# Hybrid attention layer on one core: part of the second token half's input projection goes from whole columns beside attention to seven-product blocks ahead of it, and the rest runs in held half columns

## The chip, the cores and the metric

The kernel runs on one core of a Trainium2 chip. The metric is the device time of one execution in microseconds (us). The median of three runs of the kernel before is 2537.37 us (2536.17 to 2539.38).

## The reference, cut to what matters

One layer of a streaming encoder works on 2048 tokens of width 1024, all in fp32. Its first part is what the change touches:

```python
u = rms_norm(h, g_mix_pre[l])
z = u @ w_in[l]                       # 1024 x 2816
qa, ka, va, qh, fh, ih, gh = jnp.split(z, IN_SPLITS, axis=-1)
ya = swa_with_sinks(qa, ka, va, sinks[l])     # 8 heads, sliding window of 128
yh = hgrn2(qh, fh, ih, gh, lb, onorm)         # 4 heads, gated recurrence
y = jnp.concatenate([ya, yh], axis=-1) @ w_out[l]
h = h + rms_norm(y, g_mix_post[l])
```

Cross-attention into 256 memory tokens and a SwiGLU network follow; they are not touched. The 2816 columns of `w_in` are 22 column groups of 128: 0 to 3 are `qa`, 4 `ka`, 5 `va`, 6 to 9 `qh`, 10 to 13 `fh`, 14 to 17 `ih`, 18 to 21 `gh`.

## The kernel before

**Arithmetic.** An fp32 operand is split into a rounded part and a rest (`hi`, `lo`), and each product of 128 x 128 by 128 x 512 becomes three matmuls, hi by hi, hi by lo, lo by hi (`mm3` L156 to L158, `products` L1198 to L1200). A split is a copy on ScalarE (ACT, L1035) or GpSimd (POOL, L1037) and a subtraction on VectorE (DVE, L1038).

**Blocks.** For a pair of column groups and 1024 tokens the product is a 2 x 2 block product. `plain` and `eight` form it with eight half-size products (96 matmuls of 512 columns), `seven` with seven (84), at the price of sums of the weights (`streamed`, L1173), of sums of the tokens' blocks (`resident`, keys 5, 7, 6, 4), and of sums of results. `phases` runs lists of such blocks; the token operands `T` of a list lie in seven tiles, four of the pool `big` and three of the pool `tb`, each split in two halves (`half`, `split`), and stay for the whole list.

**Stage 1, `in_first`.** The first 1024 tokens are normalised and go through the eleven pairs of `ORDER`: two plainly, nine in seven products. Beside these blocks the second 1024 tokens are normalised and stored to `un_d`. At the end they are fetched, split into four plain tiles of `big` (`u1`), and the pair (4, 5) of the second half is done plainly. `in_block.after` finishes a pair: for `fh` and `qh` (pairs (10, 6) to (13, 9)) it runs `decays` (logarithm, two scans, exponentials, L790 to L814), and then stores the pair to `z_d`, or to `zq_d`, `zk_d`.

**Stage 2, attention.** `mix` steps through three generators. `swa` does tile n's scores and softmax (`swa_front`: scores L859, L860, masked minimum on DVE L864, exponential on ACT L868, division L879) and tile n-1's output (`swa_back`: transposes L893, ACT copy L897, DVE difference L898, matmuls L902, L903). `hgrn` does the recurrence: `hgrn_last` L994, `hgrn_out` L976 and L977 (then ACT squares L981, POOL L983 and L985, DVE L986), `hgrn_state` L965, `hgrn_front` L938 (scores), POOL L946, transposes L949 and L954. `cols` (`in_proj`, `in_cols`) does the remaining 20 column groups of the second half, one per step, 48 matmuls each, with loads (`wcols`) and splits. Nine steps run all three; in the eight after them `swa` runs with `cols` and with the sums of `w_out` (`side`, DVE L1082); the rest of `cols` runs with `fold_cross`.

**PSUM.** In stage 2 there are eight banks in four kinds of two: `g` for the column groups, `s` and `t` for `swa` (with `h` from tile 8 on), and `h` for the recurrence of tiles 0 to 7. A bank is used again when its reader has finished.

**Order.** Each engine, and SyncE (SP) with the DMA issues, executes one list in order. A scheduler makes the lists when the program is built, from the order in which the code is traced and from which operands it takes to be ready; `queued(i)` puts what is traced within it behind the instruction i. So the column matmuls of `cols`, which wait for nothing but their weights, could be put anywhere between the attention matmuls.

Of the kernel before, what the change touches and what calls it, by code (L numbers as in the profile page):

```python
# [18 lines left out]
P = 128  # L19
T = 2048  # L20
# [28 lines left out]
class Layer:  # L49
# [146 lines left out]
    def mix(self):  # L196
        tc, I = self.tc, self.I
        kw = dict(reuse_waits="tile")
        with contextlib.ExitStack() as left:
# [18 lines left out]
            with tc.tile_pool(name="sw", bufs=1, side="right", **kw) as self.sw:  # L218
# [216 lines left out]

    ORDER = [(4, 5), (0, 1), (2, 3)] + [(10 + h, 6 + h) for h in range(4)] + [(c, c + 1) for c in range(14, 22, 2)]
# [31 lines left out]
    def in_first(self):  # L468
# [63 lines left out]
        second = {}  # L532

        def fetch():
            for s in range(2):
                for q in range(2):
                    r = self.pair_tile().rearrange("p a d -> p (a d)")
                    self.load(r.rearrange("p (n c) -> p n c", n=4),
                              self.un_d[4 * s:4 * s + 4, q].rearrange("n p c -> p n c"))
                    second[q, s] = r.rearrange("p (m k c) -> p k m c", m=16, k=4)  # L540
                    yield

        beside = [(), (0,), (1, 2), (3,), (4,), (5,), (6,), (7,), (), (), (), ()]
        get = fetch()
        tokens = [[] for _ in range(len(self.ORDER) + 1)]
        blocks = [("s",) + self.in_block(*p, tokens[i], tokens[i + 1], beside[i + 1], get if i > 9 else (), i < 2,
                                         None if i else lambda: x_loads(0, (2, 3)))
                  for i, p in enumerate(self.ORDER)]

# [3 lines left out]
        phases = self.phases([(lambda i, j, a, n: raw[i, j][:, a:a + n, :], 4, blocks, None, {})], T)  # L553
# [46 lines left out]
        for _ in get:  # L600
            pass
        u = []
        for s in range(2):
            u.append([])
            for q in range(2):
                self._n += 1
                t = self.big.tile([P, 2, 4, 512], F32R, tag="big", name=f"u1_{q}{s}")
                r = second[q, s]
                for k in (0, 2):
                    self.split2(r[:, k:k + 2], *(t[:, e, k:k + 2].rearrange("p k (m c) -> p k m c", m=16)  # L610
                                                 for e in range(2)), "A")
                u[s] += [(t[:, 0, k, :], t[:, 1, k, :]) for k in range(4)]

        c0 = self.ORDER[0][0] * P

        def load(t, j):
            for i, c in enumerate(self.ORDER[0]):
                self.load(t[:, :, i * P:(i + 1) * P], I["w_in"][c, :, 4 * j:4 * j + 4, :])

        stream = self.streamed(load, 4, "p")  # L620
        next(stream)
        S = list(stream)
        z, low = self.pair_tile(), self.pair_tile()
        for s in range(2):
            sl = slice(s * 512, (s + 1) * 512)
            for i in range(2):
                ps = self.bank("g")
                self.mm3(ps, [((S[i + k // 4 * 2][:, 0, k % 4, :], S[i + k // 4 * 2][:, 1, k % 4, :]), u[s][k])
                              for k in range(KT)])
                if i:  # L630
                    nc.scalar.activation(z[:, i, sl], ps, AF.Copy)
                else:
                    self.halves(c0, ps, z[:, 0, sl], low[:, 0, sl])
        self.store_halves(c0, TB, z[:, 0, :], low[:, 0, :])
        self.store(self.z_d[c0 + P:c0 + 2 * P, TB:2 * TB], z[:, 1, :])
        return u
# [13 lines left out]
    def in_block(self, ca, cb, x, ahead, beside, get, plain, between):  # L650
# [11 lines left out]
        def stream(kind):  # L662
            for _ in range(3):
                next(iter(get), None)
            return self.streamed(load, 4, kind)

        def out(i, j, a, b):
# [15 lines left out]
            if c0 < C_VA:  # L683
# [3 lines left out]
                if b is not None:  # L687
                    nc.vector.tensor_tensor(lo, a, b, ALU.add)
# [4 lines left out]
            if b is not None:  # L693
                nc.vector.tensor_tensor(zs, a, b, ALU.add)
                a = zs
            if c0 < C_QH or C_IH <= c0 < C_GH:
                if b is None:
# [11 lines left out]
        def after():  # L709
# [7 lines left out]
            if C_FH <= c0 < C_IH:  # L717
                e = self.pair_tile()
                yield from self.decays(0, (c0 - C_FH) // P, z[0][:, 0, :], e[:, 0, :], e[:, 1, :])
# [4 lines left out]
            for i, c in enumerate(() if plain else (ca, cb)):  # L724
                if c0 < C_VA:
                    self.store_halves(c * P, 0, z[1][:, i, :], z[0][:, i, :])
                else:
                    self.store(self.z_d[c * P:(c + 1) * P, 0:TB], z[0][:, i, :])
# [8 lines left out]
    def in_proj(self, b, u):  # L737

        order = [c for p in self.ORDER for c in p]
        e1 = None  # L740
        for c in order[2:]:
# [1121 lines left out]
```

## Time and profile before

| | us |
|---|---|
| median of 3 runs | 2537.37 |
| the profiled execution, its own time | 2533.9 |
| its span, first to last instruction | 2532.2 |
| busy, in the span: TensorE (PE) | 2493.8 |
| VectorE (DVE) | 1749.1 |
| ScalarE (ACT) | 1240.7 |
| GpSimd (POOL) | 365.4 |

Granted clock of TensorE: 0.998 over the span. Times in views are counted from the span's start. In them stage 1 ends at about 269 us (the blocks of the first half reach to 244.5, the plain pair of the second half to 269), attention at about 603, and `fold_cross` at about 764. A row of a timeline has start, duration, engine, line, operation, output<-input, shape, count, and in brackets the idle time before it with what ended it. A row of a group has its count after x, then the busy time in us, the mean of one in ns, and the idle time before.

### The profile page before, as it was taken

What the parts mean: (1) busy time and instruction counts of PE and PEld (TensorE: products, weight loads), DVE (VectorE), ACT (ScalarE), POOL (GpSimd) and SP (SyncE); (2) the same over time, 40 slices, a digit from 0 to 9 for tenths busy, and PEclk for the clock granted to TensorE, in tenths of its full rate; (3) what the DMA queues carried; (4) which work ended last, traced back from release to release, by engine and by line L of the source; (5) the groups of instructions that cost most, each with busy time, mean ns of one, the idle gap of its engine ahead of it and who ended that gap; (6) DMA issues with size and microseconds to landing.
All of it is one profiled execution on the core that took longest, in us unless ns stands there. A gap on an engine that the chain in (4) does not pass through costs nothing.

```text
span 2532.2 us, 33939 instructions
## 1 busy us (share of the span) xinstructions
PE 2493.8 (98%) x11942; PEld 2084.7 (82%) x11942; DVE 1749.1 (69%) x2787; ACT 1240.7 (49%) x2582; POOL 365.4 (14%) x540
## 2 busy tenths in 40 slices
PE   9999999999999999999999999999999999999998
PEld 8778888888987788878878888888888888888886
DVE  8896477865556989988866655576566557574766
ACT  5463356654565576566753333353333335443543
POOL 4241244321400111112200000000000000000122
PEclk9999999999999999999999999999999999999999
DMA  7544877785887996858944322254354334565777
GB/s 221 158 158 164 239 198 178 223 270 135 278 298 266 302 335 194 255 175 255 339 164 169 136 76 93 78 196 154 129 208 167 117 127 156 177 184 110 231 169 156
DMA packets 313403, 483.56 MB, mean 191 GB/s; under 512 B 21904, under 2 KB 198032, under 8 KB 313232
## 3 DMA queue, kind: packets, MB, share of 16 engines
q1 hardware_dynamic: 304880, 455.17, 54.1%
q0 software_dynamic: 8352, 26.22, 6.1%
q8 instruction: 94, 1.54, 0.2%
q14 instruction: 77, 0.63, 0.1%
HBM read 305.15 MB, written 176.16 MB: 190 GB/s over the span
## 4 chain that ended last, share of the span: by engine, by line
PE 83%; DVE 5%; DMA 5%; issue 2%; ACT 2%; POOL 1%; SPq 1%; DVEq 0%; POOLq 0%; ACTq 0%
PE psm L1200 22%; PE psm L1198 22%; PE psm L1199 22%; PE psg L158 2%; PE psg L156 2%; PE psg L157 2%; DVE S L1038 1%; DMA y_d<-ys 1%; DVE T L1038 1%; DMA raw<-in_wo_x_dram 1%; DVE sum L1173 0%; DMA pair<-in_x_dram 0%; DMA out_s<-u 0%; SPq L75 0%; ACT junk L1569 0%
## 5 line engine op out<-in xcount | busy, mean ns | idle before, releaser
L1198 PE MATMUL psm<-T,S 128*128 128x512 f32 x2680 | 1034.4, 391 | 12.6 <-ACT part L1213 8.4
L1199 PE MATMUL psm<-T,S 128*128 128x512 f32 x2680 | 1042.6, 390 | 1.2 <-DVE T L1038 1.1
L1200 PE MATMUL psm<-T,S 128*128 128x512 f32 x2680 | 1030.0, 390 | 5.0 <-DVE S L1038 5.0
L1198 PEld LDWEIGHTS psm<-T,S 128*128 128x128 f32 x2680 | 503.1, 188 | 124.8 <-ACT part L1213 13.0
L1200 PEld LDWEIGHTS psm<-T,S 128*128 128x128 f32 x2680 | 503.4, 188 | 112.4 <-DVE S L1038 8.4
L1199 PEld LDWEIGHTS psm<-T,S 128*128 128x128 f32 x2680 | 503.5, 188 | 106.7 <-DVE T L1038 3.0
L1035 ACT ACTIVATE S<-sum 128x512 fp32r<-128x512 f32 (+1 forms) x370 | 224.1, 619 | 374.8 <-PE psm L1200 270.4
L1038 DVE TENSOR_TENSOR S<-sraw,S 128x512 fp32r<-128x512 f32 (+1 forms) x315 | 212.0, 679 | 236.9 <-ACT S L1035 233.7
L1213 ACT ACTIVATE part<-psm 128x512 f32<-128x512 f32 x285 | 168.6, 596 | 253.1 <-PE psm L1200 237.8
L1038 DVE TENSOR_TENSOR S<-sum,S 128x512 fp32r<-128x512 f32 (+1 forms) x388 | 258.0, 673 | 43.9 <-ACT S L1035 40.0
L1035 ACT ACTIVATE S<-sraw 128x512 fp32r<-128x512 f32 (+1 forms) x300 | 184.5, 618 | 110.7 <-PE psm L1200 108.7
L1602 POOL DMA_DIRECT2D y_d<-row x16 | 14.0, 872 | 1077.3 <-DVE row L1784 1015.3
L1038 DVE TENSOR_TENSOR T<-row,T 128x1024 fp32r<-128x1024 f32 (+1 forms) x112 | 130.8, 1183 | 28.3 <-ACT T L1035 26.4
L156 PE MATMUL psg<-u,whi 128*128 128x512 f32 x320 | 127.6, 399 | 0.7 <-DVE z L770 0.5
L157 PE MATMUL psg<-u,whi 128*128 128x512 f32 x320 | 127.3, 398 | 0.0
L158 PE MATMUL psg<-u,wlo 128*128 128x512 f32 x320 | 126.7, 397 | 0.0
L1569 ACT ACTIVATE junk<-row 128x512 f32<-128x512 f32 x160 | 99.6, 624 | 46.3 <-DVE row L1591 19.9
L1035 ACT ACTIVATE T<-row 128x1024 fp32r<-128x1024 f32 (+1 forms) x112 | 113.4, 1031 | 10.6 <-DMA row<-d_s 5.3
L1735 DVE TENSOR_TENSOR row<-psm,part 128x512 f32<-128x512 f32 x66 | 44.0, 687 | 71.3 <-PE psm L1200 71.3
L1038 DVE TENSOR_TENSOR wlo<-raw,whi 128x1024 fp32r<-128x1024 f32 x52 | 65.4, 1258 | 36.0 <-ACT whi L1035 30.9
L1784 DVE TENSOR_TENSOR row<-psm,part 128x512 f32<-128x512 f32 x72 | 49.1, 687 | 49.3 <-PE psm L1200 49.2
L1744 DVE TENSOR_TENSOR part<-psm,part 128x512 f32<-128x512 f32 x66 | 43.7, 687 | 52.2 <-PE psm L1200 52.2
(355 smaller groups left out, 3476.2 us busy)
## 6 DMA issues: line engine op xcount, KB each, us to landing
sraw<-in_w_gate_dram SPq DMA_DIRECT2D x44, 512.0 KB, 3.8
sraw<-in_w_up_dram SPq DMA_DIRECT2D x44, 512.0 KB, 3.6
hid_d<-row SPq DMA_DIRECT2D x44, 512.0 KB, 2.6
sraw<-hid_d SPq DMA_DIRECT2D x32, 512.0 KB, 4.6
sraw<-in_w_in_dram SPq DMA_DIRECT2D x48, 256.0 KB, 3.9
raw<-in_w_in_dram SPq DMA_DIRECT2D x20, 512.0 KB, 6.3
row<-in_w_down_dram SPq DMA_DIRECT2D x20, 512.0 KB, 7.3
row<-d_s SPq DMA_DIRECT2D x20, 512.0 KB, 8.4
```

The source lines that it names most:

```text
L156: nc.tensor.matmul(ps, ah, bh, start=(i == 0), stop=False)
L157: nc.tensor.matmul(ps, ah, bl, start=False, stop=False)
L158: nc.tensor.matmul(ps, al, bh, start=False, stop=(i == n - 1))
L1035: self.nc.scalar.activation(hi, raw, AF.Copy)
L1038: self.nc.vector.tensor_tensor(lo, raw, f32(hi), ALU.subtract)
L1198: nc.tensor.matmul(ps, s[:, 0, k, :], t[:, 0, k, :], start=st, stop=False, **kw)
L1199: nc.tensor.matmul(ps, s[:, 0, k, :], t[:, 1, k, :], start=False, stop=False, **kw)
L1200: nc.tensor.matmul(ps, s[:, 1, k, :], t[:, 0, k, :], start=False, stop=sp, **kw)
L1213: nc.scalar.activation(t, ps, AF.Copy)
L1569: self.nc.scalar.activation(junk, a, AF.Square, scale=float(D) ** -0.5, accum_out=to)
L1735: nc.vector.tensor_tensor(d, a, c, ALU.add)
L1784: nc.vector.tensor_tensor(d, a, b, ALU.add)
```

## The change

`ORDER` and the first token half stay. A second list of blocks is handed to `phases`: the first five pairs of `ORDER` for the second half, (4, 5), (0, 1), (2, 3) and (10, 6) in seven products, and (11, 7) in eight (kind "p"). Their token operands take over the tiles of the first list one by one, each as soon as its last use there is past. Four tiles of raw tokens are fetched, and the sums 7, 5 and 6 formed, beside the last two blocks of the first half. The 12 column groups that are left use the tiles 1, 2, 8 and 3 of the last block. They run in halves of 24 matmuls: two before the first step, one in each of the first nine steps, one and two by turns in the later ones; each half after the first two is put behind the last TensorE instruction traced before it, which ends the step's `hgrn` (or `swa`).

```diff
-                for _ in range(NPB + 1):
+                next(cols)
+                for i in range(NPB + 1):
                     next(swa)
                     next(hgrn)
+                    self.hold = [self.traced(mybir.EngineType.PE)]
                     next(cols)
...
-                    next(cols)
+                    self.hold = [self.traced(mybir.EngineType.PE)]
+                    for _ in range(1 + i % 2):
+                        next(cols)
...
+    MORE = 5
...
+        more = [("p" if i == self.MORE - 1 else "s",) + self.in_block(*p, 1, (), [], (), False, None)
+                for i, p in enumerate(self.ORDER[:self.MORE])]
...
+        def sums():
+            for k, at in ((7, (1, 1)), (5, (0, 1)), (1, (0, 0)), (2, (1, 0))):
+                second[k] = fetched(*at)
+                yield
+            for d, a, b, op in ((7, 7, 5, ALU.subtract), (5, 5, 1, ALU.subtract), (6, 1, 7, ALU.add)):
...
+                for k in (0, 2):
+                    kk = slice(k, k + 2)
+                    nc.vector.tensor_tensor(second[d][:, kk], second[a][:, kk], second[b][:, kk], op)
+                    yield
...
-        phases = self.phases([(lambda i, j, a, n: raw[i, j][:, a:a + n, :], 4, blocks, None, {})], T)
+        phases = self.phases([(lambda i, j, a, n: raw[i, j][:, a:a + n, :], 4, blocks, None, {len(blocks) - 2: [sums]}),
+                              (operand, 4, more, True, {})], T)
...
-        order = [c for p in self.ORDER for c in p]
+        order = [c for p in self.ORDER for c in p][2 * self.MORE:]
...
         for s in range(TB // 512):
+            if s:
+                yield
...
-                self.mm3(ps, [((w[i][0][:, k, :], w[i][1][:, k, :]), u[s][k]) for k in range(KT)])
+                with self.queued(*self.hold):
+                    self.mm3(ps, [((w[i][0][:, k, :], w[i][1][:, k, :]), u[s][k]) for k in range(KT)])
...
+                if first and queue[0][0]:
+                    free = next(s for s in slots if s[2] == where[queue[0][1]])
```

The plain pair at the end of `in_first`, with its fetches and splits, is removed. In the program 48 matmuls of 512 columns go in all.

Two places show the new order. First TensorE, in one of the first nine steps before, from the last matmul of `hgrn_out` (L977, bank psh) on: `psg` are column matmuls, L893 transposes of the softmax, L902 its product with the values.

```order
L977 MATMUL psh_4143<-W_3880,q_3905 128x128
L893 MATMUL pst_4108<-ident,S_10_3769 128x128 x2
L893 MATMUL pst_4108<-ident,S_11_3779 128x128 x2
L157 MATMUL psg_4212<-u_10_2237,whi_4207 128x512
L158 MATMUL psg_4212<-u_10_2237,wlo_4208 128x512
L156 MATMUL psg_4240<-u_01_2242,whi_4207 128x512
L902 MATMUL pss_4102<-pth_00_4089,vst_3463 128x512
L157 MATMUL psg_4240<-u_01_2242,whi_4207 128x512
L158 MATMUL psg_4240<-u_01_2242,wlo_4208 128x512
L156 MATMUL psg_4240<-u_01_2242,whi_4207 128x512
```

Of the changed program the same engine at the end of the attention part of the same kind of step; its line numbers are nine lower in these functions (L929 are the scores of `hgrn_front`, L940 and L945 its transposes, L884 those of the softmax, L893 the product with the values).

```order
L884 MATMUL pst_4553<-ident,S_00_4240 128x128 x2
L884 MATMUL pst_4553<-ident,S_01_4250 128x128 x2
L929 MATMUL psh_4399<-qq_4394,k_4392 128x192 x2
L884 MATMUL pss_4544<-ident,S_00_4240 128x128 x2
L884 MATMUL pss_4544<-ident,S_01_4250 128x128 x2
L929 MATMUL psh_4404<-qq_4394,k_4392 128x192 x2
L940 MATMUL psh_4412<-ident,k_4392 128x128 x4
L884 MATMUL pst_4568<-ident,S_10_4273 128x128 x2
L884 MATMUL pst_4568<-ident,S_11_4283 128x128 x2
L893 MATMUL pss_4562<-pth_00_4549,vst_4002 128x512
L945 MATMUL psh_4419<-ident,v_4396 128x128 x4
L156 MATMUL psg_4426<-T_2788,whi_3985 128x512
```

The column matmuls, which lay in pieces of one to ten between the attention matmuls, now stand in one piece of 24 behind the step's last transposes; between `hgrn_out` and those there is none.

Second SP before, where attention starts: the loads of the recurrence's tile 0 and 1 (k, qq, v, sg), the store of the plain pair (`pair`), and the loads of `swa` for tile 0 (qs, kk, vr).

```order
L78 DMA zk_d<-pair_2271 128x1024
L75 DMA k_2562<-z_d 128x4x128
L75 DMA qq_2564<-z_d 128x4x128
L78 DMA z_d<-pair_2270 128x1024
L75 DMA v_2566<-z_d 128x4x128
L75 DMA sg_2771<-z_d 128x4x128
L75 DMA k_2801<-z_d 128x4x128
L75 DMA qq_2803<-z_d 128x4x128
L75 DMA qs_0_2480<-zq_d 64x4x128 x2
L75 DMA qs_1_2483<-zq_d 64x4x128 x2
L75 DMA kk_2486<-zk_d 64x4x128 x2
L75 DMA vr_2489<-z_d 128x128
```

Of the changed program the same place; `pair_2803` holds the pair (10, 6), `pair_2920` the pair (11, 7), whose columns pass through `decays`.

```order
L78 DMA z_d<-pair_2803 128x1024 x2
L75 DMA k_3229<-z_d 128x4x128
L75 DMA qq_3231<-z_d 128x4x128
L75 DMA v_3233<-z_d 128x4x128
L75 DMA sg_3403<-z_d 128x4x128
L75 DMA k_3433<-z_d 128x4x128
L75 DMA qq_3435<-z_d 128x4x128
L78 DMA z_d<-pair_2920 128x1024 x2
L75 DMA qs_0_3147<-zq_d 64x4x128 x2
L75 DMA qs_1_3150<-zq_d 64x4x128 x2
L75 DMA kk_3153<-zk_d 64x4x128 x2
L75 DMA vr_3156<-z_d 128x128
```

The loads of `swa` now follow right behind the two stores of the pair (11, 7), where four loads of the recurrence stood between the last store and them.

More of the change, by code (lines that the diff above doesn't have):

```diff
@@ L550, in in_first, with operand @@
+        def operand(i, j, a, n):
+            key = i if j is None else {v: k for k, v in self.BLOCK.items()}[i, j]
+            if key in (3, 8) and not a:
+                second[key] = fetched(i, j)
+            if key == 4:
+                return second[2][:, a:a + n], second[6][:, a:a + n]
+            return second[key][:, a:a + n]
         plain = [b[1:4] + ([],) for b in blocks[:2]]
@@ L599, in in_first @@
             pass
[L600 to L636, printed above, removed]
+        T = {k[1]: t for k, t in T.items() if type(k) is tuple and k[0]}
+        return [[(T[p][:, 0, k, :], T[p][:, 1, k, :]) for p in ps for k in range(4)] for ps in ((1, 2), (8, 3))]
     def halves(self, c0, src, hi, lo):
@@ L1346, in half @@
                 n, p, _ = k = queue.pop(0)
+                where[p] = free[2]
                 slots.remove(free)
```

72 lines of the change are left out of this document (39 added, 33 removed).

## The prediction

> **What bounds the kernel now.** I read the page first, for the span and for the engine that carries the chain that ended last.
>
> ```profile
> span 2532.2 us, 33939 instructions
> PE 2493.8 (98%) x11942; PEld 2084.7 (82%) x11942; DVE 1749.1 (69%) x2787; ACT 1240.7 (49%) x2582; POOL 365.4 (14%) x540
> PE 83%; DVE 5%; DMA 5%; issue 2%; ACT 2%; POOL 1%; SPq 1%; DVEq 0%; POOLq 0%; ACTq 0%
> ```
>
> TensorE is the bound. Next I cut the stages that the change touches into windows: the last two blocks of the first token half, the plain pair of the second half, and the attention stage in two parts. Columns: length; busy time (instructions) of PE, PEld, DVE, ACT, POOL; granted clock; DMA share; GB/s.
>
> ```profile
> 206.40:225.40 19.00, 19.00 (x86) 15.72 (x85) 9.80 (x16) 5.01 (x10) 1.86 (x3) 1.00 0.61 201
> 225.40:244.50 19.10, 18.54 (x82) 15.03 (x81) 14.64 (x19) 10.88 (x16) 2.29 (x4) 1.00 0.34 111
> 269.00:436.00 167.00, 166.34 (x976) 145.19 (x974) 108.51 (x301) 92.67 (x296) 63.36 (x100) 1.00 0.74 201
> 436.00:602.60 166.60, 165.44 (x904) 140.86 (x902) 123.02 (x309) 94.69 (x268) 44.24 (x78) 1.00 0.74 219
> ```
>
> In the attention stage PE lacks 0.66 + 1.16 us in 333.6 us: the column matmuls fill every hole of a stage whose chains run through all engines. The waits of PE from 37 to 764 us name what little is left.
>
> ```profile
> PE psm L1198 <- ACT part L1213: 6.5, 5, 3.1
> PE pst L859 <- DMA kk<-zk_d: 0.5, 1, 0.5
> ```
>
> So the change can gain by fewer matmuls, hardly by fewer waits, and loses whatever new waits it makes.
>
> **The gain.** A busy matmul is not its price, since matmuls overlap. The price is the distance of starts, from the first and last of eleven in a row:
>
> ```profile
> 261.77 0.39 PE L157 MATMUL psm<-u,S 128*128 128x512 f32 x1
> ...
> 264.03 0.39 PE L158 MATMUL psm<-u,S 128*128 128x512 f32 x1
> ```
>
> Ten steps in 2.26 us are 0.226 us each; I use 0.227. A pair of columns takes 96 such matmuls plainly and 84 in seven products, so four pairs save 48: **-10.9 us**. The fifth pair stays at 96. Nothing else leaves PE. A half column of 24 is 5.45 us.
>
> **The boundary of the halves.** The operand tiles of the second half take over the places of the first half's, step by step: 7 tiles in two halves are 14 splits, with 8 sums and differences of the same size on DVE; 8 old splits go. Their price on DVE:
>
> ```profile
> L1038 DVE TENSOR_TENSOR u<-pair,u 128x1024 fp32r<-128x1024 f32 x6 | 7.1, 1219 | 0.2 <-ACT u L1035 0.2
> ```
>
> 7.1 / 6 is 1.18 us. DVE's 24.4 us in the two windows lose 9.4, and gain most of 22 x 1.18 = 26 us; some of that reaches the first new block. About 15 + 8 + 26 = 49 us of DVE stand against 57 us of PE in three blocks: it fits on average, but the splits bunch where each tile is freed and needed one block later. Bounds: 0, as in the window of 14.64 us DVE where PE lacked 0.56; and 8, if the block that gets most work (some 27 us) holds PE for its excess over 19. I take **+3**. The new seven-product block with decays brings one more wait like the small ones under L1213: (6.5 - 3.1) / 4, **+0.9**.
>
> **The start of attention.** Swa's first loads now stand on SP behind the stores of the fifth pair, whose decays follow its last matmul, E. Before, the stores there had no such chain:
>
> ```profile
> 269.84 0.33 SPq L78 DMA_DIRECT2D z_d<-pair  x1
> ...
> 273.86 3.03 SPq L75 DMA_DIRECT2D qs<-zq_d  x4
> 276.94 1.27 SPq L75 DMA_DIRECT2D kk<-zk_d  x2
> ```
>
> ```profile
> 279.90 1.46 PE L938 MATMUL psh<-qq,k 128*128 128x192 f32 x8
> 281.07 0.53 PE L156 MATMUL psg<-u,whi 128*128 128x512 f32 x1
> 282.07 0.30 PE L859 MATMUL pst<-kk,qs 128*128 128x128 f32 x1 [0.47 <-DMA kk<-zk_d]
> ```
>
> The decays' steps, from the attention stage (ACT, then DVE):
>
> ```profile
> L790 ACT ACT_TABLE_LOAD x4 | 5.1, 1283 | 0.1
> L790 ACT ACTIVATE x<-z 128x1024 f32<-128x1024 f32 x4 | 4.2, 1061 | 0.0
> ```
>
> ```profile
> L794 DVE TENSOR_TENSOR_SCAN u<-reset,x 128x512 f32<-128x512 f32 x8 | 9.4, 1210 | 2.5 <-ACT x L790 2.5
> L800 DVE TENSOR_TENSOR u<-u,d_mid 128x1024 f32<-128x1024 f32 x4 | 4.9, 1221 | 1.0 <-POOL d_mid L798 1.0
> L814 DVE SCALAR_TENSOR_TENSOR z<-z,u 128x1024 f32<-128x1024 f32 x4 | 5.3, 1329 | 0.0
> ```
>
> Table load, logarithm, two scans, subtraction, table load, two exponentials (of the logarithm's size), product: 1.28 + 1.06 + 2.42 + 1.22 + 1.28 + 2.12 + 1.33 = 10.7, so the stores go out near E + 11. Then stores 0.7, eight qs and kk pieces 3.1 to the issue of kk, and 5.1 from that issue to the matmul (276.94 to 282.07): E + 20. PE holds two half columns (10.9) and eight score matmuls (1.2, from 279.90 to 281.07), to E + 12. That is up to 8 us; 0 if the rows overlap more than before. I take 6.5, less the 0.5 that stood there: **+6**.
>
> A wait of that length has a second price here. Behind the one long wait of this trace the starts lie farther apart:
>
> ```profile
> 113.02 0.50 PE L1198 MATMUL psm<-T,S 128*128 128x512 f32 x1 [3.15 <-ACT part L1213]
> 114.64 0.63 PE L1198 MATMUL psm<-T,S 128*128 128x512 f32 x1
> ...
> 116.77 0.63 PE L1200 MATMUL psm<-T,S 128*128 128x512 f32 x1
> ```
>
> 2.13 us for five steps are 0.426 each, for eight matmuls 1.6 us more than 0.227: **+1.6**. The Trainium skill, "TensorE: Matmul & The Clock Gate", Part 1: The HAM clock gate, has TensorE fall to half its clock after an idle window of about 3.4 us and recover after a busy one; the doubled distance agrees. By that rule waits well under a window carry no such price, by the row alone one of 3.15 us does; the sum is the same by either while waits per step stay near 1.5 us.
>
> **The held halves.** Here the sign is decided. `hold` puts each half behind the step's last attention matmul. Before, column matmuls stood between the links of the recurrence (HGRN), which has two PSUM banks ("h"). One step of it, from the tile view and the timeline:
>
> ```profile
> L977 PE MATMUL psh<-W,q x8: 274/275/275, 435.4 to 438.7; 128*128 128x128 f32 x8
> L981 ACT ACTIVATE on<-psh x4: 286/294/307, 439.1 to 439.9; 128x128 f32<-128x128 f32 x4
> L965 PE MATMUL psh<-vt,kt x8: 275/275/275, 438.8 to 439.6; 128*128 128x128 f32 x8
> L938 PE MATMUL psh<-qq,k x8: 323/326/328, 445.0 to 446.7; 128*128 128x192 f32 x8
> L949 PE MATMUL psh<-ident,k x4: 270/272/273, 452.6 to 453.0; 128*128 128x128 f32 x4
> ```
>
> ```profile
> 440.66 1.04 POOL L985 TENSOR_TENSOR h_rs<-h_vv,mhalf 128x4 f32<-128x4 f32 x1
> 441.74 0.69 DVE L986 TENSOR_TENSOR on<-psh,h_rs 128x512 f32<-128x512 f32 x1 [1.14 <-POOL h_rs L985]
> 447.90 1.58 POOL L946 TENSOR_TENSOR k<-k,G 128x256 f32<-128x256 f32 x1
> 448.26 0.28 PE L859 MATMUL pst<-kk,qs 128*128 128x256 f32 x1
> ...
> 448.61 0.28 PE L860 MATMUL pst<-kk,qs 128*128 128x256 f32 x1
> ```
>
> The bank of `out` comes free at 442.4, 3.4 us after its last matmul ended (439.0); the scores that reuse such a bank ran at 445.0. In the new order stand between them 16 score matmuls (0.117 each, 1.9), two of 512 (0.45), the state (eight in the trace, 0.9) and four transposes (0.4): 3.6 us against 3.4, with nothing left for a queue, and DVE's `on` now stands behind four masked minima. The k transposes wait for POOL's product: 447.0, where the scores end, to 449.5, 2.5 us against 0.4 of other work, or 1.5 with the 1.04 us that POOL's other operations took. So a step waits between 0.3 (all smooth) and 3.5 us (both, and DVE late); I take 1.5, near the second link alone. Eight steps: **+12**. The eight later steps have no recurrence; their chain per step is transposes, ACT copy, DVE difference, with six banks: 0 to 0.75 each, **+2**.
>
> DVE's load rises with it: 384 matmuls (87.2 us) leave the stage of 333.6, and of its 231.5 us of DVE some 25 go (eight splits at 1.2, the decays of two columns at 5.0 each by the rows above, and an estimated 5 of small work): 206 of 246, 84%, where the second window has 74%.
>
> That PE cannot step over such a wait is seen at 282.07: it stood for kk while the column of 281.07 was half done and its other matmuls lay behind. The Trainium skill, same page, Architectural detail, says the same: only weight loads are pulled ahead, matmuls keep the program's order. Could PE reorder, the held halves would fill the waits and these 14 us would be 0.
>
> **Sum.** -10.9 + 3 + 0.9 + 6 + 1.6 + 12 + 2 = +14.6. The profiled execution took 2533.9 us (span 2532.2), which gives 2548.5; it lies 3.5 under the median 2537.4, so I forecast **2552**.
>
> **Rivals.** *Covered (faster):* the half columns, 5.45 us each, let DVE, ACT and POOL run ahead, so that a step's chains are ready when it comes. For it: PE was never late at 74% DVE. Only the start then costs 1 or 2: 2537.4 - 10.9 + 1.5 = 2528. It decides if a step waits under 0.3 us and the first kk comes before E + 14. Chance 0.21.
> *Cancelled:* start, clock and boundary cost 10 to 12, the steps little: 2537. Chance 0.17.
> *DVE bound:* in the first nine steps decays and the sums of w_out come on top; each step waits 3.5: 2552 + 16 = 2568 or more. Against it: the average of 84%. Chance 0.12.
> *Half clock in the steps:* waits of a step join into one as long as at 113.02; 8 x 1.6 = 13 more, 2565. No wait of the attention stage of this trace is that long; the Trainium skill's rule named above would need an idle window each step. Chance 0.08.
> *Forecast:* 2543 to 2563, chance 0.42.
>
> **Numbers.** About 0.2% (5 us) is what a measurement of this kernel can tell from no change: 2532.3 to 2542.4. Faster 0.21, same 0.17, slower 0.62. The lower bounds of all terms give -10.9 + 0.9 + 2.4, 2530; the upper -10.9 + 8 + 0.9 + 8 + 1.6 + 28 + 6, 2579. For 8 in 10 I take 2528 to 2574.
>
> **What would show it.** Right: 48 matmuls fewer at 0.227; a PE wait of 5 us or more for kk where attention starts, with matmuls 0.43 apart behind it; waits of PE psh for L977 (`on`) and for POOL's k in the first nine steps, 8 to 20 us together; the 24 column matmuls of a half without a hole. Wrong: an attention stage of 246 us with PE at 99%, or waits that fall on PE in the blocks instead.

## The result, and the profile after

The changed kernel takes 2582.66 us (median of 4 runs, 2581.18 to 2583.41) against 2536.89 us (4 runs, 2536.17 to 2539.38): ratio 1.0178, 95% interval 1.016 to 1.0196. It is slower by 45.8 us; the forecast was 2552, 14.6 us slower, in 2528 to 2574, so the side was right, the size was too small by two thirds, and the time lies above the range. Lines of `mix` and below are nine lower than before: L850 and L851 are the scores, L855 the masked minimum, L884 the transposes, L888 the ACT copy, L889 the DVE difference, L893 and L894 the products with the values, L929, L940, L945 the recurrence's scores and transposes.

The page of the changed kernel, its span, busy times and chain:

```profile
span 2581.1 us, 33987 instructions
PE 2510.8 (97%) x11894; PEld 2089.7 (81%) x11894; DVE 1788.1 (69%) x2851; ACT 1265.1 (49%) x2617; POOL 374.3 (15%) x544
PE 78%; DVE 7%; DMA 5%; ACT 3%; issue 3%; POOL 2%; SPq 0%; DVEq 0%; POOLq 0%; ACTq 0%
```

The 48 matmuls are gone (11942 to 11894), and still PE is busy for 17 us longer and its share of the last chain falls from 83% to 78%; DVE's and ACT's rise.

Then the windows of the blocks where the halves meet, of the changed kernel (length; busy time and instructions of PE, PEld, DVE, ACT, POOL; granted clock; DMA share; GB/s):

```profile
225.00:244.00 19.00, 18.22 (x81) 14.75 (x80) 14.45 (x22) 9.95 (x15) 2.28 (x3) 1.00 0.44 146
244.00:263.00 19.00, 18.18 (x79) 14.32 (x78) 18.49 (x24) 12.06 (x17) 5.49 (x3) 1.00 0.35 125
```

Two blocks lack 0.8 us each. DVE is full in the second (18.49 of 19.00), and it is enough. From the start of attention (269.0 before, 348.5 after) the boundary's price follows: 79.5 us, less the 336 matmuls that came forward (384 less 48) at 0.227, 76.3, leaves 3.2.

Now the attention stage, first its nine steps with the recurrence, then the eight without:

```profile
348.50:517.00 168.50, 145.37 (x859) 126.03 (x858) 122.50 (x326) 99.34 (x317) 70.31 (x109) 0.95 0.85 242
517.00:656.50 139.50, 129.04 (x660) 104.01 (x658) 83.65 (x262) 72.52 (x223) 29.11 (x55) 0.96 0.56 144
```

PE lacks 23.1 and 10.5 us where it lacked under 2 in all, and its clock is 0.95 and 0.96 where it was 1.00. The stage holds 504 column matmuls where it held 864; with 360 fewer at 0.227 the 333.5 us before would be 252 with no new wait, and it takes 308.0. Behind it nothing was lost: from its end to the span's end it was 2532.2 - 602.5 = 1929.7 before and is 2581.1 - 656.5 = 1924.6 now, with 24 column matmuls fewer left over (72 for 96, 5.4 us).

A stage whose column work changes can't be compared by its length. The next view counts the column matmuls alone (tiles psg; PE's busy time and count come second; 4 of the 868 before are scores of the recurrence in that bank, which is under 1 us), of the kernel before:

```profile
269.00:453.50 184.50, 119.04 (x451) 82.02 (x450) 8.19 (x12) 10.72 (x18) 1.00 0.73 198
453.50:602.50 149.00, 103.77 (x417) 76.07 (x417) 5.83 (x9) 10.92 (x19) 1.00 0.75 224
```

and of the changed kernel:

```profile
348.50:517.00 168.50, 52.70 (x217) 40.70 (x217) 2.72 (x4) 5.26 (x9) 0.95 0.85 242
517.00:656.50 139.50, 67.26 (x288) 53.77 (x288) 3.43 (x5) 7.16 (x12) 0.96 0.56 144
```

Length less count x 0.227 is what attention and recurrence take of PE's time beside the columns, waits and slow clock with them. I call it the rest. Before: 184.5 - 102.4 = 82.1 and 149.0 - 94.7 = 54.3, together 136.4. After: 119.2 and 74.1, together 193.3. So the whole loss is 57 us in this rest: -10.9 + 3.2 + 56.9 = 49.2, against 48.9 between the two spans. The rest is the measure for all runs below; a busy column doesn't show it, because a matmul that stands alone is busy for 0.39 us and in a row costs 0.227.

The waits of PE from 348 to 657 us, changed kernel (us in total, times, longest):

```profile
PE pss L884 <- DVE w_mn L855: 5.2, 5, 1.9
PE pst L884 <- DVE w_mn L855: 4.5, 9, 2.4
PE pst L850 <- DVE w_mn L855: 4.3, 2, 3.0
PE pst L850 <- DMA kk<-zk_d: 4.3, 1, 4.3
PE psh L893 <- ACT pth L888: 3.9, 7, 1.9
PE pss L894 <- DVE ptl L889: 3.1, 2, 2.0
PE psh L940 <- POOL d_g L802: 1.9, 1, 1.9
```

One row is the start (kk). L940, the k transposes, is of the recurrence: one wait of 1.9 for GpSimd's d_g, and none of the rows is for its normed output. The others are links inside window attention: minima, the copies and differences of the softmax weights.

The start, in the timeline of PE (start, duration, ..., idle before):

```profile
359.24 1.46 PE L929 MATMUL psh<-qq,k 128*128 128x192 f32 x8
365.02 0.45 PE L850 MATMUL pst<-kk,qs 128*128 128x128 f32 x1 [4.32 <-DMA kk<-zk_d]
...
370.31 0.63 PE L158 MATMUL psg<-T,wlo 128*128 128x512 f32 x1
370.74 0.63 PE L156 MATMUL psg<-T,whi 128*128 128x512 f32 x1
371.93 0.39 PE L156 MATMUL psg<-T,whi 128*128 128x512 f32 x1
```

The wait of 4.32 us, and behind it 0.43 between starts until 371.9: 6.9 us at about half clock, which is some 3.4 us lost. Start and clock cost 4.3 + 3.4 = 7.7.

A held half, in the same timeline:

```profile
529.07 0.48 PE L156 MATMUL psg<-T,whi 128*128 128x512 f32 x1
...
534.41 0.40 PE L158 MATMUL psg<-T,wlo 128*128 128x512 f32 x1
...
539.48 0.33 PE L832 MATMUL pss<-ident,vr 128*128 128x128 f32 x1 [0.26 <-DVE w_mn L855]
540.29 0.66 PE L884 MATMUL pst<-ident,S 128*128 128x128 f32 x4 [0.48 <-DVE w_mn L855]
```

24 matmuls in a piece, the first start at 529.07 and the last at 534.41, without a hole; then attention alone, with gaps of some tenths between its groups.

### The profile page after: what moved, and what is told of

The parts are those of the page before. It is cut to its first block, busy times and chain, and to the rows that moved or that the text cites. A ratio compares the mean times of both kernels' runs of the same rounds, so it can differ in the third digit from the quotient of the medians.

```text
span 2581.1 us, 33987 instructions
## 1 busy us (share of the span) xinstructions
PE 2510.8 (97%) x11894; PEld 2089.7 (81%) x11894; DVE 1788.1 (69%) x2851; ACT 1265.1 (49%) x2617; POOL 374.3 (15%) x544
## 4 chain that ended last, share of the span: by engine, by line
PE 78%; DVE 7%; DMA 5%; ACT 3%; issue 3%; POOL 2%; SPq 0%; DVEq 0%; POOLq 0%; ACTq 0%
PE psm L1196 22%; PE psm L1194 22%; PE psm L1195 22%; DVE T L1029 1%; PE psg L156 1%; PE psg L157 1%; PE psg L158 1%; DVE S L1029 1%; DVE S L855 1%; ACT junk L1571 1%; POOL pair L689 1%; DMA pair<-in_x_dram 0%; DVE sum L1169 0%; PE psh L157 0%; PE psh L156 0%
## 5 line engine op out<-in xcount | busy, mean ns | idle before, releaser
L1194 PE MATMUL psm<-T,S 128*128 128x512 f32 x2824 | 1090.2, 391 | 16.1 <-ACT part L1209 9.7
L1195 PE MATMUL psm<-T,S 128*128 128x512 f32 x2824 | 1099.5, 390 | 1.8 <-DVE T L1029 1.6
L1196 PE MATMUL psm<-T,S 128*128 128x512 f32 x2824 | 1086.2, 390 | 4.0 <-DVE S L1029 4.0
L1194 PEld LDWEIGHTS psm<-T,S 128*128 128x128 f32 x2824 | 530.9, 188 | 135.1 <-ACT part L1209 14.4
L1196 PEld LDWEIGHTS psm<-T,S 128*128 128x128 f32 x2824 | 531.0, 188 | 117.2 <-DVE S L1029 7.0
L1195 PEld LDWEIGHTS psm<-T,S 128*128 128x128 f32 x2824 | 531.0, 188 | 113.9 <-DVE T L1029 4.6
L1029 DVE TENSOR_TENSOR S<-sraw,S 128x512 fp32r<-128x512 f32 (+1 forms) x327 | 220.6, 681 | 234.9 <-ACT S L1026 231.9
L1209 ACT ACTIVATE part<-psm 128x512 f32<-128x512 f32 x297 | 175.8, 596 | 264.0 <-PE psm L1196 247.0
L1029 DVE TENSOR_TENSOR S<-sum,S 128x512 fp32r<-128x512 f32 (+1 forms) x404 | 269.1, 675 | 45.3 <-ACT S L1026 40.4
L1029 DVE TENSOR_TENSOR wlo<-raw,whi 128x1024 fp32r<-128x1024 f32 x44 | 54.0, 1227 | 51.0 <-ACT whi L1026 35.4
L1786 DVE TENSOR_TENSOR row<-psm,part 128x512 f32<-128x512 f32 x72 | 49.1, 688 | 49.0 <-PE psm L1196 48.9
L1169 DVE TENSOR_TENSOR sum<-sraw,sraw 128x512 f32<-128x512 f32 (+1 forms) x101 | 69.3, 686 | 14.6 <-DMA sraw<-in_w_in_dram 10.7
L156 PE MATMUL psg<-T,whi 128*128 128x512 f32 x192 | 76.4, 398 | 0.0
L158 PE MATMUL psg<-T,wlo 128*128 128x512 f32 x192 | 75.4, 393 | 0.0
```

What stands on the lines that cost most here:

```text
L156: nc.tensor.matmul(ps, ah, bh, start=(i == 0), stop=False)
L158: nc.tensor.matmul(ps, al, bh, start=False, stop=(i == n - 1))
L1029: self.nc.vector.tensor_tensor(lo, raw, f32(hi), ALU.subtract)
L1169: nc.vector.tensor_tensor(t, a, b, op)
L1194: nc.tensor.matmul(ps, s[:, 0, k, :], t[:, 0, k, :], start=st, stop=False, **kw)
L1195: nc.tensor.matmul(ps, s[:, 0, k, :], t[:, 1, k, :], start=False, stop=False, **kw)
```

## The experiments

Theory: the hold takes the filler away from the holes, in every step. Rivals: the attention stage has too little column work left, held or not; VectorE or its transfers bind; the start or the boundary costs the difference. Each edit is against the changed kernel unless it says otherwise. "Rest" is given for the first nine and the last eight steps.

**1. No hold.**

```diff
-                    self.hold = [self.traced(mybir.EngineType.PE)]
```

(in both places)

> The changed kernel without the hold: the column matmuls of the twelve groups may again stand anywhere between the attention matmuls; everything else as changed. Theory H (the held halves leave the attention chains uncovered): nearly all of the 57 us that were lost beside the 10.9 gained come back but for the late start, 2530 to 2540. Theory F (too little column work is left for the stage, so DVE, ACT and the DMAs bound it in any order): 2570 to 2590. Theory S (DVE stands in its list for the DMAs of the w_out sums): unchanged, 2575 to 2585.

Measured: 2560.78 us (2560.26 to 2562.56), ratio to the kernel before 1.0095 (1.008 to 1.011). The time lies between the ranges of all three theories. The hold is worth 21.9 us, and without it 24 us are still lost. Its column matmuls:

```profile
348.50:538.00 189.50, 111.79 (x434) 78.30 (x432) 3.40 (x5) 10.46 (x18) 1.00 0.85 241
538.00:645.00 107.00, 30.69 (x122) 22.06 (x122) 4.40 (x7) 3.21 (x6) 0.94 0.60 149
```

Rest 91.0 and 79.3. The free columns ran ahead: 434 of them in the first nine steps, where 217 ran with the hold, and only 122 were left for the last eight. There PE waits as under the hold. So two causes, not one.

At the start the order of the free halves matters too. The first scores run at the same time as under the hold (365.02), but PE has column matmuls until then, and no wait for kk stands there; the clock is 1.00 over the first nine steps. The longest wait on a load is a later one:

```profile
365.36 0.22 PE L848 MATMUL pst<-kk,qs 128*128 128x128 f32 x1
PE pss L830 <- DMA vr<-z_d: 1.8, 1, 1.8
```

With one more of 1.1 us, PE waits for 2.9 us up to 380, where it lost 7.7 under the hold.

**2. The hold at full column work.** One plain pair ahead, twenty column groups left, two halves a step, held, and the same without the hold.

```diff
-    MORE = 5
+    MORE = 1
...
-                    next(cols)
+                    for _ in range(2):
+                        next(cols)
...
-                    for _ in range(1 + i % 2):
+                    for _ in range(2):
```

> MORE = 1: only the pair (4, 5) goes ahead, in plain, so that 20 column groups are left as before the change; they run in halves, two per step, each held. 48 matmuls more than changed. Theory H: each of 17 steps waits as in the changed kernel, 2575 to 2595. Theory F: the column work covers the stage as before, 2537 to 2545. Theory S: the stage is long enough for the DMAs, 2537 to 2550.

> Control for the run with one plain pair and two held halves a step (2598.37 us): the same twenty columns, the same two halves a step, no hold. Theory 'the hold costs by itself': 2535 to 2540 us, as the kernel before, so that the hold is worth about 60 us at the full column work. Rival 'it is the cutting into halves or the new writing of the block products that costs there': 2570 us or more without the hold too.

Measured: held 2598.37 us (2597.29 to 2602.24), ratio 1.0245 (1.023 to 1.026); free 2545.71 us (2543.59 to 2550.19), ratio 1.0039 (1.0023 to 1.0054). 52.7 us between them, with the same matmuls: 3.1 us in each of 17 steps. The held one lies 3 us above the range of the theory that the hold costs in each step, and 48 us or more above those of the two others. The free one was expected at 2540 or less; its loss of some 8 us lies in the blocks ahead of attention, which starts at 277.0 in place of 269.0 with the same number of matmuls ahead of it; in the last 40 us of these blocks PE is busy for 35.78 (39.44 in the kernel before). Column matmuls of the held one, then of the free one:

```profile
277.00:474.50 197.50, 91.98 (x385) 73.03 (x385) 8.24 (x12) 9.58 (x16) 0.97 0.68 183
474.50:657.50 183.00, 101.77 (x432) 82.50 (x432) 4.09 (x6) 10.74 (x18) 0.95 0.64 186
```

```profile
277.00:461.00 184.00, 118.88 (x451) 81.81 (x450) 8.18 (x12) 10.72 (x18) 1.00 0.76 202
461.00:613.50 152.50, 103.81 (x417) 76.08 (x417) 5.85 (x9) 10.92 (x19) 1.00 0.74 221
```

Rest 110.1 and 84.9 held, 81.6 and 57.8 free: the hold costs 28 us in nine steps and 27 in eight, 3.2 and 3.4 a step. The eight steps without a recurrence are no cheaper.

**3. The hold in the first nine steps alone, and in the last eight alone.**

In the loop of the last eight, for the first of the two runs:

```diff
-                    self.hold = [self.traced(mybir.EngineType.PE)]
+                    self.hold = []
```

In the loop of the first nine, for the second:

```diff
-                    self.hold = [self.traced(mybir.EngineType.PE)]
```

> The changed kernel with the hold in the first nine steps alone; the halves of the last eight steps are free. The hold of all seventeen steps was worth 21.9 us (2582.66 against 2560.78). By the working of the forecast (12 us of the hold's price in the first nine steps, 2 in the last eight) nearly all of it stays: 2579 to 2582 us. Theory 'the hold costs in every step alike, since each step has holes that only column work fills': half of it goes, 2566 to 2574 us.

> The changed kernel with the hold in the last eight steps alone. By the working of the forecast nearly nothing of the hold's price is left: 2560 to 2565 us. Theory 'every step alike': 2566 to 2574 us. Together with its twin the two parts should add up to about 22 us over the kernel with no hold (2560.78).

Measured: first nine held 2562.14 us (2561.13 to 2565.79), ratio 1.0102 (1.0084 to 1.012); last eight held 2582.9 us (2580.77 to 2583.2), ratio 1.0183 (1.0167 to 1.0199). Both expectations missed: the hold of the last eight steps carries the whole price, that of the first nine none. Column matmuls, first nine held, then last eight held:

```profile
348.50:514.50 166.00, 52.47 (x216) 40.49 (x215) 2.72 (x4) 5.25 (x9) 0.96 0.87 245
514.50:647.50 133.00, 84.97 (x340) 61.90 (x340) 5.08 (x8) 8.59 (x15) 1.00 0.59 158
```

```profile
348.50:517.00 168.50, 67.56 (x264) 48.12 (x263) 2.73 (x4) 6.36 (x11) 0.96 0.86 248
517.00:654.00 137.00, 55.78 (x240) 45.12 (x241) 3.43 (x5) 5.96 (x10) 0.96 0.54 140
```

| held | rest, first nine | rest, last eight | together |
|---|---|---|---|
| nowhere | 91.0 | 79.3 | 170.3 |
| first nine | 117.0 | 55.8 | 172.8 |
| last eight | 108.6 | 82.5 | 191.1 |
| all | 119.2 | 74.1 | 193.3 |
| before (20 groups, free) | 82.1 | 54.3 | 136.4 |

With twelve groups the columns cover one part of the stage or the other. A hold in the first nine steps costs 26 us there (some 5 of it at the start, 7.7 for 2.9) and gives 24 back, since the halves it keeps cover the last eight (55.8, about as before the change). A hold in the last eight gives nothing back: its halves can no longer run ahead into the first nine steps (91.0 grows to 108.6), and placed behind the last steps they cover none. The smallest of the four sums is the shortage, 34 us over the kernel before (with the 2.9 us of waits at the start); the hold at the end adds 21, that of the first nine 2.

**4. Held, but behind the attention step before.**

```diff
-                    self.hold = [self.traced(mybir.EngineType.PE)]
+                    self.hold, late = late, [self.traced(mybir.EngineType.PE)]
```

(in both loops, `late` empty at first)

> The changed kernel, but each half is held behind the attention step before the one it is written after, so that one step's column work may fill that step's own holes and still can't run ahead by more than a step. Theory 'the hold puts the filler behind the holes': the holes of 1 to 3 us in the steps are filled, and the column work lasts to the end; 2540 to 2552 us, clearly below the changed kernel without any hold (2560.78). Rival 'twelve columns are too little to cover sixteen steps, wherever they stand': 2558 to 2566 us, as without a hold. Rival 'VectorE and its transfers bind there': 2570 to 2582 us.

Measured: 2566.22 us (2560.53 to 2570.66), ratio 1.0123 (1.0106 to 1.014); the profiled execution lies at the low end of these.

```profile
346.00:511.00 165.00, 61.92 (x240) 44.13 (x239) 2.73 (x4) 5.89 (x10) 0.97 0.87 248
511.00:642.50 131.50, 76.69 (x307) 55.82 (x308) 4.06 (x6) 7.08 (x12) 1.00 0.59 152
```

Rest 110.5 and 61.8, together 172.3: as much as with no hold (170.3) and as with the hold in the first nine (172.8). Three ways to place the twelve groups, one sum. Spreading doesn't make up for the missing work; of the three expectations the second fits, the median 0.2 us above its range.

**5. Sixteen groups left, free.**

```diff
-    MORE = 5
+    MORE = 3
...
-                    self.hold = [self.traced(mybir.EngineType.PE)]
-                    next(cols)
+                    for _ in range(2):
+                        next(cols)
```

(one half ahead of the first step, and no hold in the last eight either)

> Only two column pairs in seven products and one in plain, sixteen columns left for the attention, in halves, none held: 24 matmuls fewer than the kernel before, which are 5.4 us. Theory 'what the changed kernel loses without its hold is the shortage of column work near the end': with 32 halves in place of 24 there are 44 us more of it, so that the last 30 us of the steps stand uncovered and not the last 77: 2533 to 2542 us. Rival 'the block products of the second half cost something of their own that no column work covers': 2548 us or more.

Measured: 2555.3 us (2550.12 to 2557.77), ratio 1.0072 (1.0055 to 1.0088). The first theory missed: I thought that cover ends only where the columns end. The time lies in the rival's range, but the blocks' own cost is a small part: attention starts 40.5 us later than before, and the 168 matmuls more ahead of it are 38.1 at 0.227, which leaves 2.4.

```profile
309.50:502.00 192.50, 111.89 (x422) 77.36 (x421) 5.42 (x8) 10.08 (x17) 0.99 0.78 213
502.00:638.00 136.00, 83.01 (x326) 60.50 (x326) 5.19 (x8) 8.50 (x15) 0.99 0.67 190
```

Rest 96.7 and 62.0, together 158.7. So with free halves the rest grows as they become fewer: 139.5 with 40 (experiment 2), 158.7 with 32, 170.3 with 24. Each step down moves two pairs more into seven products, which saves 5.4 us of matmuls, and adds 12 to 19 us to the rest. The medians follow: 2545.7, 2555.3, 2560.8. In this series no further pair pays, and none of its members comes below the kernel before.

**6. The start.** The five pairs in another order, those with decays first, (2, 3) plainly last.

```diff
-                for i, p in enumerate(self.ORDER[:self.MORE])]
+                for i, p in enumerate(self.ORDER[3:self.MORE] + self.ORDER[:3])]
```

> The changed kernel, its five column pairs of the second half in another order: the two with decays first, (2, 3) in plain last, so that no decay stands between the last products and attention's first loads. Theory 'the wait of 4.3 us for the keys and the half clock behind it come from the decays and stores of pair (11, 7)': the wait goes, 5 to 8 us less, 2574 to 2578 us. Rival 'the keys wait for the stores of the last pair, whichever it is': 2581 to 2584 us, the wait still 3 us or more.

Measured: 2593.1 us (2588.72 to 2595.24), ratio 1.0221 (1.0206 to 1.0237): slower still, where 5 to 8 us less was expected. A wait of PE stayed at the same place:

```profile
PE pst L850 <- DMA qs<-zq_d: 3.7, 1, 3.7
```

It is now named by the first load of SP's list and no longer by the third. The first scores run 16.1 us after the columns' first matmul (355.0 to 371.1), in the changed kernel 16.7 (348.35 to 365.02). So it isn't the decays of (11, 7) that make the loads late; and by experiment 1, with (11, 7) last and no hold, the lateness needn't cost the 4.3 us: it costs them where the held halves leave PE nothing else. With the decays at the other end of the list the blocks wait more: 8.1 us in four rows between 250 and 300 us, the longest of them

```profile
PE psm L1194 <- DVE pair L681: 3.3, 1, 3.3
```

where the changed kernel has one row of 0.8 there. Attention starts at 355 us in place of 348.5; the rest of its stage, 193.6, is that of the changed kernel (193.3), so the loss lies ahead of it.

**7. Where in a step.** Each half of the first nine steps held behind `swa` of its step, not behind `hgrn`; and, apart from it, bank g given to `swa` as well.

```diff
                     next(swa)
+                    self.hold = [self.traced(mybir.EngineType.PE)]
                     next(hgrn)
-                    self.hold = [self.traced(mybir.EngineType.PE)]
```

```diff
-                swa = self.swa(range(NT), lambda n: "st" if n < NPB else "sth")
+                swa = self.swa(range(NT), lambda n: "stg" if n < NPB else "sthg")
```

> The changed kernel, each half of the first nine steps held behind the window attention of its step and no longer behind the recurrence of the same step, so that it may fill the recurrence's holes. By the links that the forecast named (the bank of the normed output and GpSimd's product before the k transposes, both in the recurrence) most of the price of these steps goes: 2568 to 2574 us. Theory 'the holes are in the window attention (minima, softmax, the rest of the weights), not in the recurrence': 2577 to 2583 us, the same waits.

> The changed kernel, its window attention given PSUM bank g beside the banks that it had; g is the column halves' bank and stands idle while they are held. Theory 'TensorE waits for VectorE's minima only because the two score banks are not free yet': the waits of the scores on the minima (14 us in the three rows) fall by half or more, 2568 to 2576 us. Rival 'VectorE itself is late, and another bank moves the wait to the transposes behind it': within 4 us of the changed kernel, 2578 to 2586 us.

Measured: 2585.45 us (2582.78 to 2587.28), ratio 1.0192 (1.0173 to 1.021), and 2601.08 us (2598.86 to 2604.26), ratio 1.0258 (1.0241 to 1.0274). The first is no faster although the halves may now stand in the recurrence; it lies 2.5 us above the second theory's range. Its three longest waits of PE in total:

```profile
PE pst L884 <- DVE w_mn L855: 6.7, 8, 2.5
PE psh L893 <- ACT pth L888: 4.9, 9, 2.0
PE psh L956 <- DVE sg L986: 4.7, 2, 3.3
```

The first two, and most of the smaller rows, are in window attention, where the waits were in the changed kernel; the third, the recurrence's state (L956) behind DVE, is new. So filling the recurrence gains nothing, and it brings a wait of its own. With the third bank PE's waits on the minima fall from 14.0 to 4.2 (3.7 of it in the row below), but the wait of the k transposes for POOL grows:

```profile
PE psh L940 <- POOL k L937: 10.1, 4, 5.9
PE pss L884 <- DVE w_mn L855: 3.7, 5, 1.4
```

and the kernel is 18 us slower, which neither theory had. The bank was a limit for the waits on the minima; with it free the lists are others, and in them the k transposes stand before POOL is ready. What part of the 18 us is that, and what part the bank that columns and `swa` now share, these runs don't tell.

**8. The sums of w_out.** They run on DVE, with loads and stores, in both kernels beside attention. They are put behind it, in the changed kernel and in the kernel before.

```diff
-                    for _ in range(4):
-                        next(side, None)
+                self.mark()
+                with self.queued(self.traced(mybir.EngineType.PE)):
+                    for _ in side:
+                        pass
```

(and the single `next(side)` goes)

> The changed kernel, with DVE's eight sums of w_out put behind the last attention step instead of between the steps. Theory S: most of the loss in the stage goes, 2540 to 2555. Theory H: the sums are a small part, 2572 to 2580. Theory F: about 10 us of DVE less in the stage, 2570 to 2575.

> Control: the kernel before with the same move of the w_out sums. All theories: 2534 to 2540, since its attention stage has no waits; a slower time would be the price of the sums in the place where they now stand.

Measured: 2575.86 us (2575.15 to 2577.16), ratio 1.0154 (1.0139 to 1.0169), and 2549.19 us (2548.08 to 2551.8), ratio 1.0047 (1.003 to 1.0063). The first lies in Theory H's range, the control above the 2534 to 2540 expected. The move gains 6.8 in the changed kernel and costs 12.7 in the kernel before, where the sums were free and now stand on the path. The sums disturb the changed kernel by about 6.8 + 12.7 = 19.5 us, if their price behind attention is the same in both. Column matmuls of the changed kernel with the sums behind:

```profile
348.50:502.00 153.50, 52.54 (x216) 40.49 (x215) 2.73 (x4) 5.26 (x9) 0.97 0.79 211
502.00:639.00 137.00, 67.68 (x288) 53.92 (x288) 3.41 (x5) 7.18 (x12) 0.99 0.54 139
```

Rest 104.5 and 71.6 against 119.2 and 74.1: 15 of 17 us come out of the first nine steps. That is where the sums ran: the code writes them into the last eight steps, but in the changed kernel's trace they start between 447.2 and 507.4 us, before the first nine end at 517. They are 10.1 us of DVE work, and DVE stood idle for another 8.5 before them, for their loads and stores; how the price divides between that standing and the transfers, no run here takes apart.

**9. More VectorE work.** 68 operations of 128x512 on a tile of their own, four a step, in the changed kernel and in the kernel before.

```diff
+                    with self.queued(self.traced(mybir.EngineType.DVE)):
+                        for _ in range(4):
+                            self.nc.vector.tensor_tensor(scr, scr, scr, ALU.min)
```

> The changed kernel with four more VectorE operations of 128x512 in each of the seventeen steps, on a tile of their own, written behind the step's own VectorE work: 68 in all, some 0.6 us each by the nearest rows (a subtraction of 128x512, ptl, took 0.60 us), so 41 us of VectorE work that nobody waits for. Theory 'VectorE's list binds the uncovered steps': the steps grow by half of that or more, 2602 to 2625 us. Rival 'each step is bound by the length of its chain (scores, minima, exponentials, weights, transposes, products), and VectorE has room beside it': 2583 to 2595 us.

> The control: the kernel before with the same 68 operations. TensorE has column work for every hole there: theory 'twenty free columns cover VectorE's lateness': 2537 to 2545 us. Rival 'VectorE is at its limit in these steps with full column work too': 2555 us or more.

Measured: 2595.87 us (2594.28 to 2596.97), ratio 1.0236 (1.0221 to 1.0251), and 2534.79 us (2529.63 to 2537.51), ratio 0.9989 (0.998 to 0.9999). What was added, in the changed kernel:

```profile
L226 DVE TENSOR_TENSOR scr<-scr x68: 651/684/1433, 361.8 to 672.5; 128x512 f32<-128x512 f32 x68
```

46.5 us more on VectorE cost 13.2 in the changed kernel, between the two ranges expected and 1 us above the rival's, and nothing in the kernel before. So VectorE's list is part of the steps' length, by 28% of what is put on it, but it doesn't bind alone; that the remainder is the length of the step's chain is what is left, and is argued, not shown. At 28% the 10.1 us of the sums of experiment 8 would cost some 3 us (an estimate), not 15, so most of their price lies in the standing or the transfers. And with twenty free groups even 46 us of lateness are covered: that is what the change gave away.

## Why the prediction was wrong

**The gain, -10.9: right.** 48 matmuls, 0.227 apart.

**The boundary, +3 and +0.9: right.** 3.2 measured, with DVE full in one block.

**The start, +6 and +1.6: size right by luck, cause half wrong.** 4.3 of wait and 3.4 of clock make 7.7: the wait was shorter and the clock's price twice as large, and the two misses cancel. "whose decays follow its last matmul" isn't the cause: with the decays elsewhere a wait of 3.7 us stayed (experiment 6). That two half columns and eight scores are all that PE has until the loads land was right, and it is the part that costs: with free halves the wait for kk is gone (experiment 1).

**"Eight steps: +12": this step failed.** The first nine steps' rest grew by 37.1, of which 7.7 are the start: 29 in place of 12. The two links that I priced, the bank of the normed output and POOL's product, don't show among PE's long waits of the changed kernel (the k transposes wait once, 1.9 us, for another operation of POOL), and filling the recurrence gains nothing (experiment 7). PE waits mostly for links in window attention, which the step's working left out: minima, copies, differences. I had counted the matmuls that still stood between two events of the recurrence and not asked the same of the chain beside it.

**"The eight later steps ... 0 to 0.75 each, +2": this step failed most.** 19.8 measured, ten times the term. By the table of experiment 3 it is the hold on these steps' halves that costs, 21 us, and without any hold their rest is no smaller (79.3); at full column work they lose 3.4 us each to it, as much as the others (experiment 2). So a step needs no recurrence to be expensive.

**What the working lacked.** Both terms asked what the hold does. None asked what it means that 384 of 960 column matmuls leave a stage that needs them as cover. The first view had it: PE lacked 1.8 us in 333.6 because the columns filled every hole. Of the 56.9 us that the rest grew, 170.3 - 136.4 = 33.9 come without any hold, 31 of them beyond the 2.9 us of waits at the start, and 23 with it, some 5 of these at the start. In the rival *Covered* I let half columns of 5.45 us carry the steps; their number was the question, not their length.

**The rivals.** *Covered* and *Cancelled* fell. *DVE bound* had the size (3.5 us a step, 2568 or more), and a part of the mechanism: the sums of w_out do disturb the first nine steps, by 15 us. As a bound it fell in experiment 9. *Half clock in the steps* is there, though I gave it a chance of 0.08: of the stage's windows of 3.41 us eight have a clock of 0.50, two of them the start's, and PE is busy for 25.9 us in them. At half speed that is at most 13 us of the 57, 9.5 of them behind the start (an estimate from the windows). It is a consequence of the waits; no run here takes it apart from them.

**What stays open:** how the 3 us of a step divide among the links of its chain, and why a third bank makes it worse by 18 us; and what part of the price of the sums of w_out is their transfers.

## What to carry to other kernels

Work that waits for nothing is cover, and its price is not its own duration: before taking it out of a stage to do it more cheaply, subtract from the stage what it takes (length less count times spacing), and ask what that rest would be with less of it. Here two pairs saved 5.4 us of matmuls and added 12 to 19 us of waits and slow clock beside them. An order that keeps filler for later pays only if there are holes later; held behind the last steps it fills none.

## What the runs showed of the hardware

In the attention stage TensorE fell to half clock without one long wait. Four windows of the changed kernel:

```profile
501.40:504.80 3.40, 3.24 (x28) 2.97 (x27) 0.54 (x1) 1.31 (x9) 0.00 (x0) 1.00 1.08 301
504.80:508.30 3.50, 1.23 (x8) 1.02 (x8) 2.11 (x2) 1.09 (x2) 1.29 (x2) 1.00 0.63 208
508.30:511.70 3.40, 1.91 (x9) 1.91 (x10) 2.67 (x8) 1.09 (x4) 3.22 (x4) 0.51 0.94 321
511.70:515.20 3.50, 3.50 (x12) 2.97 (x11) 2.24 (x5) 1.47 (x4) 1.35 (x3) 0.50 0.73 221
```

In the second PE was busy for 1.23 of 3.50 us, in eight instructions; its waits around them were 1.48 and 2.43 us. The third and fourth ran at half clock, after 515.2 it was back. The stage has five such falls behind the start's, each after a window of 3.41 us in which PE was busy for 1.23 to 1.75 us; after two windows with 1.55 and 1.71 the clock stayed at 1.00, so the busy time alone doesn't tell them apart. The Trainium skill, "TensorE: Matmul & The Clock Gate", Part 1: The HAM clock gate, speaks of an idle window of about 3.4 us before the clock falls and of a busy one before it returns; the return agrees, while the fall came here behind a stretch that was a third busy, with no wait of 3.4 us in it. By that rule the forecast had let short waits go free of this price.
